# Holding each store that follows a load until the store ahead of it has landed on all DMA engines

## The chip, the cores and the metric

The kernel runs on one core of a Trainium2 chip. The metric is the device time of one execution in microseconds (us), lower is better.

## The reference, cut to what matters

```python
# q, k: (16 batches, 512 positions, 16 heads, 64) float32; cos, sin: (512, 32)
q_rot = concat([q1*cos - q2*sin, q1*sin + q2*cos], axis=-1)   # k_rot likewise
scores = np.einsum('bshd,bthd->bsht', q_rot, k_rot)           # (16, 512, 16, 512) float32
```

The output is 268.4 MB and the two inputs together are 67.1 MB. The arithmetic is small beside that, so the kernel is a stream of transfers with some matrix products behind it.

## The kernel before

One batch gives four stores of 4 MB each (128 positions x 16 heads x 512 columns), and needs one 2 MB load of q and one of k. All of them are issued by SyncE, in one queue, in the order store, q load, store, k load, store, store. Each store is split over 16 DMA engines (8 packets of 32 KB on each), each load likewise (8 packets of 16 KB).

```python
in_pool    = ctx.enter_context(tc.tile_pool(name="in", bufs=2))
stage_pool = ctx.enter_context(tc.tile_pool(name="stage", bufs=3))   # 3 x 4 MB: the stores' sources
...
def load(which, b):
    ...
    nc.sync.dma_start(t.rearrange("p c (h d) -> p c h d", h=H), dram[which][b])
...
def store(i, st):
    o = o_v[i // C, i % C]
    if i < NST - 1:
        nc.sync.dma_start(o, st)
        return
    ...                                # the last store of all goes in three pieces
...
for i in range(C, NST):                # C = 4 stores a batch, NST = 64 stores
    ...
    st = stage_pool.tile([P, H, S], fp32, tag="stage", name="st")
    for p in range(HP):
        scores(i, p, st)               # matmuls, copy to st; the last p calls store(i, st)
        ...
    if i % C == C - 2:
        load("q", i // C + 2)
    elif i % C == C - 1:
        load("k", i // C + 3)
```

In the text, s0 to s3 are the four stores of a batch. The q load is issued behind s2, the k load behind s3; so s3 follows the q load, and the next batch's s0 follows the k load.

## Time and profile before

| | before |
|---|---|
| median of 3 runs | 801.04 us (800.56 to 801.60) |
| profiled execution | span 799.0 us, clock 0.923 |
| bytes | 67.24 MB read, 268.44 MB written |
| DMA queue of the stores and loads | busy 98.6% of 16 engines' time |

The first two lines below are from the profile's page of the kernel before, its part on DMA issues: what is issued, how often, its size, and the median time from issue to landing. The last one is the page's row of GB/s in 40 equal slices of the span.

```profile
out_dram<-st SPq DMA_DIRECT2D x59, 4096.0 KB, 23.9
k_sb<-in_k_dram SPq DMA_DIRECT2D x15, 2048.0 KB, 26.9
...
GB/s 355 422 424 424 432 427 433 425 435 427 421 437 426 439 427 430 433 431 430 431 428 433 434 428 429 433 438 420 418 426 434 435 415 418 426 440 375 422 439 231
```

A 4 MB store at 432 GB/s takes 9.7 us, so a time to landing of 23.9 us means that a store stands behind more than a whole other transfer. The row of GB/s is even, 415 to 440 from the second slice to the 36th, and ends in a slice with 231: there some DMA engines have finished and others have not. The first and the last of the 16 DMA engines are 8.9 us apart at the end. This distance is called the **lead** here. The engine that is last sets the time.

Under these views lie two sorts of records. A transfer leaves 16 completion marks, one for each DMA engine; "first marks" and "last marks" below are the earliest and the latest of the 16. And each packet has a start and a duration. Where numbers come from these, the text says so, and tables made from them stand in ordinary fences.

### The profile page before, as it was taken

To read this page: it belongs to the slowest core of one execution; us is meant where nothing else is said; L and a number is where in the kernel's file an instruction comes from. 1 tells how busy PE (TensorE), PEld (TensorE's weight loads), DVE (VectorE), ACT (ScalarE), POOL (GpSimd) and SP (SyncE) were. 2 spreads that over 40 slices of the span, in tenths; PEclk is the share of its full clock that TensorE was granted. 3 is DMA by queue.
4 is the path that set the end of the run, shared out by engine and by line. 5 is a ranking of instruction groups with operands and counts; after the bars stand their busy time and mean duration, and the time that the engine had idled before them with its cause. 6 is when DMAs were issued, how large, how long until landed. Compare 5 with 4: busy or idle time off the path is not lost.

```text
span 799.0 us, 7715 instructions
## 1 busy us (share of the span) xinstructions
PE 691.3 (87%) x3072; PEld 299.3 (37%) x3072; DVE 544.6 (68%) x516; ACT 561.2 (70%) x647; POOL 0.7 (0%) x6
## 2 busy tenths in 40 slices
PE   4989998997979979799797997979979799799970
PEld 2444443343434334343343443424434343344420
DVE  6999987676866768577585775857758478585300
ACT  3888886775857758577585775757757677578870
POOL 0000000000000000000000000000000000000000
PEclk9999999898998989889898898988989899899995
DMA  9999999999999999999999999999999999998995
GB/s 355 422 424 424 432 427 433 425 435 427 421 437 426 439 427 430 433 431 430 431 428 433 434 428 429 433 438 420 418 426 434 435 415 418 426 440 375 422 439 231
DMA packets 17844, 336.17 MB, mean 421 GB/s; under 512 B 1808, under 2 KB 3088, under 8 KB 4240
## 3 DMA queue, kind: packets, MB, share of 16 engines
q1 hardware_dynamic: 17520, 335.55, 98.6%
q8 instruction: 24, 0.39, 0.2%
q10 hardware_dynamic: 288, 0.13, 0.1%
q14 instruction: 12, 0.10, 0.0%
HBM read 67.24 MB, written 268.44 MB: 420 GB/s over the span
## 4 chain that ended last, share of the span: by engine, by line
DMA 50%; PE 40%; ACT 4%; DVE 3%; issue 1%; ACTq 0%; SPq 0%; DVEq 0%
DMA out_dram<-st 47%; PE ps L166 30%; PE bank L127 10%; ACT st L173 4%; DMA q_sb<-in_q_dram 2%; DVE part L106 1%; DMA early<-in_k_dram 1%; DVE q_sb L107 0%; DVE k_sb L107 0%; DVE k_sb L111 0%; DVE q_sb L111 0%; DVE early L107 0%; DVE kT_t L142 0%; ACTq L281 0%; DVE early L111 0%
## 5 line engine op out<-in xcount | busy, mean ns | idle before, releaser
L173 ACT COPY st<-ps 128x1024 f32<-128x1024 f32 x512 | 494.7, 1018 | 203.7 <-DMA out_dram<-st 105.6
L166 PE MATMUL ps<-kT_t,qT_t 64*128 64x512 f32 x2048 | 548.9, 654 | 71.0 <-ACT st L173 70.9
L166 PEld LDWEIGHTS ps<-kT_t,qT_t 64*128 64x128 f32 x2048 | 185.0, 197 | 261.7 <-issue 144.6
L142 DVE COPY qT_t<-bank 128x512 f32<-128x512 f32 x118 | 81.6, 691 | 203.8 <-PE bank L127 203.8
L127 PEld LDWEIGHTS bank<-ident,q_sb 128*128 128x128 f32 x480 | 55.6, 152 | 102.5 <-issue 99.1
L127 PE MATMUL bank<-ident,q_sb 128*128 128x128 f32 x480 | 86.9, 308 | 0.9 <-PE ps L166 0.9
L127 PEld LDWEIGHTS bank<-ident,k_sb 128*128 128x128 f32 x480 | 50.5, 141 | 95.4 <-issue 38.7
L127 PE MATMUL bank<-ident,k_sb 128*128 128x128 f32 x480 | 78.7, 287 | 1.6 <-DVE qT_t L142 1.2
L142 ACT COPY kT_t<-bank 128x512 f32<-128x512 f32 x122 | 72.5, 599 | 6.4 <-PE bank L127 6.4
L107 DVE TENSOR_TENSOR q_sb<-q_sb,cos_t 128x1024 f32<-128x1024 f32 x60 | 73.5, 1226 | 2.1
L111 DVE TENSOR_TENSOR k_sb<-k_sb,part 128x1024 f32<-128x1024 f32 x60 | 73.5, 1225 | 2.1
L107 DVE TENSOR_TENSOR k_sb<-k_sb,cos_t 128x1024 f32<-128x1024 f32 x60 | 73.5, 1225 | 2.0
L106 DVE TENSOR_TENSOR part<-q_sb,ss_t 128x1024 f32<-128x1024 f32 x60 | 73.5, 1225 | 2.0
L106 DVE TENSOR_TENSOR part<-k_sb,ss_t 128x1024 f32<-128x1024 f32 x60 | 73.0, 1216 | 0.1
L111 DVE TENSOR_TENSOR q_sb<-q_sb,part 128x1024 f32<-128x1024 f32 x60 | 73.0, 1216 | 0.0
L127 PE MATMUL bank<-ident,early 128*128 128x128 f32 x64 | 10.5, 316 | 12.5 <-DVE early L111 10.6
L127 PEld LDWEIGHTS bank<-ident,early 128*128 128x128 f32 x64 | 8.3, 161 | 17.5 <-issue 13.4
L106 DVE TENSOR_TENSOR part<-early,ss_t 128x1024 f32<-128x1024 f32 x8 | 9.8, 1223 | 5.9 <-DMA early<-in_k_dram 5.8
L111 DVE TENSOR_TENSOR early<-early,part 128x512 f32<-128x512 f32 x16 | 10.3, 687 | 0.2
L107 DVE TENSOR_TENSOR early<-early,cos_t 128x1024 f32<-128x1024 f32 x8 | 9.8, 1225 | 0.3
L142 ACT COPY qT_t<-bank 128x512 f32<-128x512 f32 x10 | 5.7, 617 | 3.2 <-PE bank L127 3.2
L142 DVE COPY kT_t<-bank 128x512 f32<-128x512 f32 x6 | 4.1, 685 | 0.3 <-PE bank L127 0.3
(9 smaller groups left out, 2.8 us busy)
## 6 DMA issues: line engine op xcount, KB each, us to landing
out_dram<-st SPq DMA_DIRECT2D x59, 4096.0 KB, 23.9
k_sb<-in_k_dram SPq DMA_DIRECT2D x15, 2048.0 KB, 26.9
q_sb<-in_q_dram SPq DMA_DIRECT2D x15, 2048.0 KB, 29.9
out_dram<-st SPq DMA_DIRECT2D x16, 1024.0 KB, 14.3
out_dram<-st SPq DMA_DIRECT2D x1, 3584.0 KB, 20.4
early<-in_k_dram SPq DMA_DIRECT2D x1, 1536.0 KB, 8.9
early<-in_q_dram SPq DMA_DIRECT2D x1, 1536.0 KB, 12.1
early<-in_k_dram SPq DMA_DIRECT2D x1, 512.0 KB
```

Source lines behind the costliest of these rows:

```text
L106: nc.vector.tensor_tensor(pv, xs, ss, op=mult)
L107: nc.vector.tensor_tensor(xc, xc, cs, op=mult)
L111: nc.vector.tensor_tensor(y, y, z, op=add)
L127: nc.tensor.transpose(bank[:, x, :], src, ident)
L142: copy(out=dst, in_=src)
L166: nc.tensor.matmul(out=po, lhsT=lhs[64 * r : 64 * r + 64, :], rhs=rh, start=True, stop=True)
L173: nc.scalar.copy(out=so, in_=si)
```

## The change

The intent: the fast DMA engines run ahead of the slow one; if a store that follows a load waits until the store ahead of that load has landed on all 16, the lead can't grow, and the load that lies between keeps the slow engine busy during the wait. Nothing else is changed: 24 stores (s3 and s0 of batches 2 to 13) get one more condition.

```diff
+    HELD = [x for x in range(2 * C, NST - 2 * C) if x % C in (0, C - 1)]
...
+    stores = {}
+    held = mybir.DependencyInfo(mybir.DependencyClass.Sync, mybir.DependencyReason.ANTI)
+
     def store(i, st):
         o = o_v[i // C, i % C]
         if i < NST - 1:
-            nc.sync.dma_start(o, st)
+            stores[i] = nc.sync.dma_start(o, st)
+            if i in HELD:
+
+                tc.add_manual_dep(stores[i].ins, stores[i - 1].ins.name, held, reason="lead")
             return
```

## The prediction

> **What bounds the kernel now.** I read the page's strip of 40 slices and its DMA queues first, to see whether the transfers or the compute engines are full.
>
> ```profile
> PE   4989998997979979799797997979979799799970
> ...
> DMA  9999999999999999999999999999999999998995
> ...
> q1 hardware_dynamic: 17520, 335.55, 98.6%
> ```
>
> TensorE has holes (7s), the DMA row has none until slice 37. The transfers of the one queue take 98.6% of the time of 16 DMA engines: 335.55 MB in 799 us. So I asked next for the stretches (start:end, span of the stretch, then busy time of each engine; the last three numbers are the granted clock, the DMA share and GB/s).
>
> ```profile
> 400.00:600.00 200.00, 178.12 (x778) 75.96 (x778) 138.60 (x130) 141.10 (x162) 0.00 (x0) 0.91 1.00 429
> ...
> 730.00:780.00 50.00, 43.91 (x196) 18.25 (x194) 13.93 (x16) 39.12 (x43) 0.00 (x0) 0.97 0.98 420
> 780.00:799.00 19.00, 0.00 (x0) 0.00 (x0) 0.00 (x0) 0.00 (x0) 0.00 (x0) 0.56 0.57 236
> ```
>
> The middle is full of DMA (share 1.00). In the last 19 us nothing computes and only 57% of the DMA engines' time is used: some engines are done before others. That is the "lead" that the change speaks of. The timeline of the queue that issues the transfers shows one period (start, duration, what is issued), and the chain of waits shows what a period hangs on:
>
> ```profile
> 433.00 0.33 SPq L147 DMA_DIRECT2D out_dram<-st  x1
> 433.43 1.00 SPq L79 DMA_DIRECT2D q_sb<-in_q_dram  x1
> 449.23 0.33 SPq L147 DMA_DIRECT2D out_dram<-st  x1
> 449.66 0.56 SPq L79 DMA_DIRECT2D k_sb<-in_k_dram  x1
> 459.25 10.35 SPq L147 DMA_DIRECT2D out_dram<-st  x2
> ```
>
> ```profile
> 408.91 28.12 DMA out_dram<-st
> ...
> 437.12 1.02 ACT st L173
> 438.14 0.04 issue
> 438.19 2.08 PE ps L166 x4
> ...
> 458.21 1.02 ACT st L173
> 459.23 0.02 issue
> 459.25 27.26 DMA out_dram<-st
> ```
>
> A period is store, q load, store, k load, store, store. A 4 MB store lands 28.12 us after its issue, of which it needs about 10 to move: the rest it stands in line. Its landing frees one of three stage buffers, ScalarE and TensorE refill it, and the next store is issued at 459.25, long before the DMA engines can start it. The wait view says the same from the queue's side and from ScalarE's:
>
> ```profile
> SPq L147 <- ACT st L173: 657.0, 59, 16.6
> ...
> ACT st L173 <- DMA out_dram<-st: 105.6, 28, 6.0
> ```
>
> The queue is waiting for data 657 us in total, ScalarE waits 105.6 us for buffers, and neither leaves the DMA engines empty.
>
> Then I went below these views, to the trace's 16 completion marks of each transfer, one for each DMA engine, and to its packets. Three facts, all mine from those records:
> - The first and the last mark of a transfer drift apart: 3.67 us at the store issued at 73.85, 5.47 at 210.78, 9.19 at 408.91, 11.75 at 630.97, and 8.91 at the store issued at 777.43. Near the end, one engine alone makes most of it: of the store issued at 616.90 the last mark is 11.45 us after the first, the one before it 5.42.
> - Between stores the first marks are 9.68 us apart, the last ones 9.83 to 10.01; for a load it is about 4.86 us for the last mark. Of 6,251 full 32 KB packets between 100 and 700 us, most took 1.213 us. Those between 1.216 and 1.30 us follow each other without a gap nearly all the time: one DMA engine, about 34 ns longer in each of the eight packets of a store (0.27 us a store).
> - Four stores and two loads on the slow engine: last marks at 437.02 and 486.51, 49.5 us apart. 4 x 9.96 + 2 x 4.86 = 49.6. So **the slow engine is never empty, and its work is the end of the kernel**.
>
> **What the Trainium skill says.** "DMA: Bandwidth & Descriptors", section "Why a DMA increments its semaphore by 16 and not by 1": the engines of one DMA finish independently, and only the full 16 means that all has landed. The trace agrees: 16 marks, up to 11.75 us apart. The same page, "Anatomy of one DMA": a DMA engine does not wait on a semaphore, the wait happens on the issuing sequencer before dispatch, and a DMA has a fixed cost of about 2 us. The first holds here (the queue's waits above); the fixed cost measures less: the store issued at 740.24 found an engine just run dry and its first mark came at 751.19, 10.95 us later; less 9.68 of moving that is 1.27 us, of which 0.48 lie between the end of the last packet (436.54) and the mark (437.02). Same page, "Where 436 GB/s comes from": 16 ports give 435 GB/s, 27.2 each. 32 KB in 1.213 us is 27.0 GB/s: the fast engines run at their own ceiling, so slowing them down hands nothing obvious to the slow one.
>
> **The change part by part.** It removes and moves no instruction; the order on every engine is the same. It adds one condition to 24 stores (two of each batch, stores 8 to 55): the whole landing of the store before.
> 1. *What the queue waits.* In the kernel before, a store after a q load was ready a mean of 7.9 us, and one after a k load 12.8 us, before the last mark of the store ahead (nine of each whose marks are complete). So all 24 will really be held: 12 x 7.9 + 12 x 12.8 = 248 us of waiting on the issuing queue. In that time the queue would mostly have waited for ScalarE.
> 2. *What the slow engine sees.* When the last mark comes, it has the 2 MB load queued already (issued 0.43 us after the store, some 24 us before it is needed). It needs 4.86 us for it. From its last packet's end to the first packet of the held store: 0.48 (mark) + 0.8 (the rest of the 1.27) + some 0.1 of waking = 1.4 us. Reserve: 4.86 - 1.4 = about 3.5 us. **No bubble on the slow engine**: cost 0 of 24 x 1.4 = 34 us.
> 3. *What the fast engines see.* They finish the load ahead of the slow one and run dry if their lead is over about 3.5 us. So the lead is cut to about 3.5 us at each held store. They lose up to 10 us once in the course of the run, which they lose in the kernel before too: in the tail, and at about 550 and 650 us, where the lead fell from 11.7 to 10.0.
> 4. *What follows behind.* The k load, issued right after the held store, slips by 8 us, but stands behind that store anyway. The store after a held one: I drew the buffers by hand, with the landing of the batch's first store as 0. Landings 0, 10, 20, 35, 50, 60, 70; a buffer is refilled 10 us after it comes free; the store that lands at 60 is ready at 30 and may be issued at 35, the one that lands at 70 at 45. Both are there well before 50 and 60. Cost 0.
> 5. *What could be gained.* The slow engine's excess: 63 large stores x 0.27 = 17 us at the very most, an estimate. But its excess does not grow with the lead: it is there at 83 us already, with a lead of 3.7. It follows TensorE instead: a mean of 12 ns a packet where TensorE was busy under a quarter of the packet's time, 35 ns where it was over three quarters; and 39 against 30 ns with over half of the engines in a load against none. The change thins such overlap out: at most 87 packets x 10 ns = 0.9 us.
>
> Sum: 801.04 + 0 - 0.5 = **800.5 us**.
>
> **The rivals.** *(a) The lead itself makes the slow engine slow*, so cutting it gives back up to its excess; for it speaks the tail with 43% of the DMA time empty, against it that the excess is there at small leads. It would make 788 to 796 us; I give it one in ten. *(b) The held stores leave the slow engine empty*, because waking, issuing and starting take longer than one load: each microsecond over 4.86 costs 24 us. A wait of 6 us would make 828. Against it the 1.27 us measured; one in twenty-five. *(c) TensorE or ScalarE becomes the bound* as buffers come free later: 178 us of 200 busy leaves TensorE 11%, and buffers come free with the slow engine as before. Under 2%.
>
> **Range and chances.** My case leaves 0 to 1 us of gain; run to run the kernel moves by 0.5. For (a) in part I go down to 794, for a little of (b) up to 805. Over 2% faster means under 785, which needs nearly all of the slow engine's excess gone: 0.03. Over 2% slower, over 817, needs 0.7 us of emptiness at every held store: 0.03. The rest, 0.94, is the same.
>
> **What would show each step.** (1) The queue's wait view: a new line, stores waiting for stores, about 24 times and 200 to 250 us. (2) Issue to landing: held stores at about 15 us (4.86 - 0.5 + 10), k loads at about 19 instead of 26.9, q loads still near 30; the DMA share in the middle still about 1.0. (3) First and last mark of a transfer never much over 4 us apart at held stores, growing by some 2 us in the last eight stores. (5) Last marks still 9.9 to 10.0 us apart between stores. The prediction is wrong if the last marks move to 9.7 us (rival a), or if packets on the slow engine show gaps before held stores (rival b).

## More of the kernel before

The marks of each transfer are told apart by counting them off from the front, 16 for each; only the last two, small transfers leave fewer. So a mean over the 12 batches rests on all twelve, of the one execution that was profiled.

## The result, and the profile after

| | before | after |
|---|---|---|
| median of 6 runs | 801.11 us (800.17 to 801.68) | 806.02 us (805.08 to 806.95) |
| ratio | | 1.0062 (95%: 1.0049 to 1.0075) |
| profiled span, clock | 799.0 us, 0.923 | 804.7 us, 0.925 |

The first three of the six runs before are those of the table above. A ratio is the mean time of one kernel's fast runs over the mean of the other's fast runs of the same rounds, so it is not quite the ratio of the medians quoted. The changed kernel is 4.9 us, or 0.6%, slower. By the 2% rule that is "the same", but it lies outside the predicted range, and the interval excludes zero.

**The page after.** The rows are the DMA busy tenths and the GB/s in 40 slices, the share of the queue, and the issue-to-landing medians.

```profile
DMA  9999999999999999999999999999999999999997
GB/s 358 423 424 429 435 424 422 417 429 433 404 435 415 418 437 398 435 420 414 424 410 431 418 417 433 403 433 423 410 429 404 431 419 416 430 421 424 437 426 301
...
q1 hardware_dynamic: 17520, 335.55, 99.1%
...
out_dram<-st SPq DMA_DIRECT2D x59, 4096.0 KB, 21.2
k_sb<-in_k_dram SPq DMA_DIRECT2D x15, 2048.0 KB, 19.7
q_sb<-in_q_dram SPq DMA_DIRECT2D x15, 2048.0 KB, 28.6
```

The change did what it was meant to do: the last slice has 301 GB/s where it had 231, so the engines finish closer together, and the DMA queue is busier than before (99.1% against 98.6%). Yet the same bytes took longer. Busy DMA engines that move less: between the second slice and the 36th, the row of GB/s has dips to 398 to 410 that the kernel before doesn't have. It isn't emptiness but slowness, and that is the reading to take from this page.

**The stretches after** (start:end, span, busy time of PE, PEld, DVE, ACT, POOL; then clock, DMA share, GB/s).

```profile
100.00:400.00 300.00, 266.59 (x1164) 113.81 (x1164) 208.60 (x196) 211.84 (x243) 0.00 (x0) 0.91 1.00 422
...
400.00:600.00 200.00, 173.48 (x776) 74.37 (x774) 136.76 (x129) 140.46 (x163) 0.00 (x0) 0.92 1.00 421
...
780.00:804.70 24.70, 0.94 (x6) 0.11 (x2) 0.00 (x0) 2.50 (x3) 0.00 (x0) 0.62 0.78 329
```

In the middle, 421 GB/s at a DMA share of 1.00; before, the stretch 400 to 600 had 429, also at 1.00. In the tail, 78% of the DMA engines' time is used, before it was 57%.

**The queue's timeline after** (start, duration, issue), one period, and **the chain of waits after** over the same time:

```profile
409.64 0.33 SPq L151 DMA_DIRECT2D out_dram<-st  x1
410.08 1.91 SPq L80 DMA_DIRECT2D k_sb<-in_k_dram  x1
424.48 9.45 SPq L151 DMA_DIRECT2D out_dram<-st  x3
434.03 1.14 SPq L80 DMA_DIRECT2D q_sb<-in_q_dram  x1
459.86 0.33 SPq L151 DMA_DIRECT2D out_dram<-st  x1
```

```profile
385.17 24.41 DMA out_dram<-st
...
409.64 14.77 DMA out_dram<-st
424.42 0.02 issue
...
433.59 26.20 DMA out_dram<-st
...
459.86 14.74 DMA out_dram<-st
```

The store issued at 409.64 is a held s3; it lands 14.77 us later, and only then, at 424.48, the held s0 goes out, together with two that had been ready. In the chain of before a store took 27 to 28 us from issue to landing; now the held ones take 14.5 to 15.6, by the marks of all 24.

**The queue's waits and ScalarE's, after** (who waits for whom: us in total, times, longest):

```profile
SPq L151 <- DMA out_dram<-st: 446.2, 24, 24.6
SPq L151 <- ACT st L180: 214.6, 25, 11.3
```

```profile
ACT st L180 <- DMA out_dram<-st: 114.2, 33, 6.6
```

The first line is the change: 24 waits of a store for a store. The two lines together are 660.8 us, where the kernel before waited 657.0 for ScalarE alone: the hold lies inside a wait that was there already. Counted from the end of the last copy into a store's buffer to the store's issue, the 24 holds come to 271 us (before: under 1 us). ScalarE waits 8.6 us longer for its buffers.

**Where the time went.** The last marks, from the trace, give the speed of the engine that sets the end. The table has the mean distance from the last mark of one transfer to the last mark of the next, in us, and in brackets the same for the first marks:

```
            q load       s3            k load        s0           s1           s2            period
before   4.91 (4.91)  9.97 ( 9.87)  4.93 (5.03)  9.89 (9.70)  9.82 (9.68)  10.01 ( 9.68)  49.53 (48.88)
after    5.07 (4.94)  9.90 (10.33)  5.33 (5.06)  9.86 (9.77)  9.86 (9.69)   9.90 (10.15)  49.94 (49.95)
```

The four stores together became 0.17 us faster on the last engine (39.70 to 39.53), the two loads 0.57 us slower (9.84 to 10.41), 0.41 of it in the k load. The sum, 0.40 us a period, times 12 periods is 4.8 us of the 5.2 by which the last mark of the last held store (store 55) comes later (719.46 before, 724.68 after); the other 0.4 us was there at store 7, before the first hold. The last mark of the last store's large piece is 5.24 us later. So nearly all of it was lost before the tail, and nothing came back in the tail although the lead there is 5.5 us instead of 8.9: a shorter lead let the fast engines finish later, not the slow one earlier.

**What happens at a load.** The rate of all engines in half-microsecond steps, worked out from the packets, at the same place of both kernels:

```
us         418.0  418.5  419.0  419.5  420.0  420.5  421.0  421.5  422.0
before       431    430    432    431    432    432    432    432    433   GB/s
after        431    431    343    324    322    311    379    425    428   GB/s
```

At 419 the changed kernel's engines, which the hold had made run dry and then released together at 410, finish the held store and turn to the k load. Eleven packets of 32 KB that start between 419.02 and 419.68 take 1.4 to 2.4 us each where 1.21 is usual. The view of stretches shows the same dip; the first two lines are the kernel before, the last two the changed one:

```profile
419.00:421.00 2.00, 2.00 (x12) 0.72 (x8) 1.35 (x3) 0.00 (x0) 0.00 (x0) 1.00 1.12 483
421.00:423.00 2.00, 0.20 (x2) 0.00 (x0) 1.00 (x1) 0.67 (x1) 0.00 (x0) 1.00 1.08 467
...
419.00:421.00 2.00, 2.00 (x12) 1.11 (x12) 1.97 (x2) 1.76 (x4) 0.00 (x0) 1.00 1.03 328
421.00:423.00 2.00, 2.00 (x13) 0.81 (x9) 1.42 (x2) 0.82 (x1) 0.00 (x0) 1.00 1.02 434
```

This view counts a packet, its time and its bytes, where it starts, so in stretches as short as these only the ratio of GB/s to share tells how fast packets move: 483 / 1.12 = 431 before, 328 / 1.03 = 318 after, and 434 / 1.02 = 425 two us later. Nobody is idle, many are slow. The two kernels differ in step, too: before, the fast engines read while the slow ones still write (at 419.0, 234 GB/s of reads and 198 of writes). After, ten of the stretched packets start within 0.15 us of each other.

The slow engines themselves are hit later: at 624.49 the held s0 goes out, the fast engines start it together at about 625.7, and of the three or four engines that are still in their k load, seven packets take 0.7 to 1.4 us instead of 0.61 between 625.5 and 627.7. In the twelve batches in order the k load's last mark is 4.82, 4.87, 4.85, 5.82, 5.50, 5.39, 5.63, 5.15, 5.56, 5.41, 5.65 and 5.33 us after the store's: not in the first three, and in all nine from store 19 on. Loads are now and then this long without any hold, too, in the first third of a run: a q load of 5.55 and a k load of 5.27 in the kernel before. What makes those long is open.

### The profile page after: what moved, and what is told of

Its sections match the earlier page's. It is cut to its first block, busy times and chain, and to the rows that moved or that the text cites. A ratio compares the mean times of both kernels' runs of the same rounds, so it can differ in the third digit from the quotient of the medians.

```text
span 804.7 us, 7713 instructions
## 1 busy us (share of the span) xinstructions
PE 688.3 (86%) x3072; PEld 298.3 (37%) x3072; DVE 544.5 (68%) x516; ACT 561.5 (70%) x647; POOL 0.7 (0%) x6
## 3 DMA queue, kind: packets, MB, share of 16 engines
q1 hardware_dynamic: 17520, 335.55, 99.1%
## 4 chain that ended last, share of the span: by engine, by line
DMA 60%; PE 26%; DVE 5%; ACT 5%; issue 1%; ACTq 0%; SPq 0%
DMA out_dram<-st 59%; PE ps L173 20%; PE bank L128 7%; ACT st L180 5%; DVE part L107 2%; DVE early L112 1%; DVE k_sb L112 1%; DVE k_sb L108 1%; DVE early L108 1%; DMA sin_t<-in_sin_dram 0%; DVE kT_t L143 0%; DVE q_sb L108 0%; DVE q_sb L112 0%; ACT kT_t L143 0%; ACTq L288 0%
## 5 line engine op out<-in xcount | busy, mean ns | idle before, releaser
L128 PE MATMUL bank<-ident,early 128*128 128x128 f32 x64 | 10.5, 316 | 12.3 <-DVE early L112 10.4
## 6 DMA issues: line engine op xcount, KB each, us to landing
k_sb<-in_k_dram SPq DMA_DIRECT2D x15, 2048.0 KB, 19.7
q_sb<-in_q_dram SPq DMA_DIRECT2D x15, 2048.0 KB, 28.6
```

What stands on the lines that cost most here:

```text
L128: nc.tensor.transpose(bank[:, x, :], src, ident)
```

## The experiments

Twelve kernels ran, all with right results. Edits are against the changed kernel except where the text says so. Times before are those of the same rounds.

### two_back: the condition without its bite

```diff
-                tc.add_manual_dep(stores[i].ins, stores[i - 1].ins.name, held, reason="lead")
+                tc.add_manual_dep(stores[i].ins, stores[i - 2].ins.name, held, reason="lead")
```

> The same 24 stores are held, but for the landing of the store two before them, which in the kernel before had landed 2 us or more ahead of their issue. The wait stands in the program and never binds. Theories A, B and C: no change, 800.5 to 801.7, leads of 8 to 12 us as before. If the added semaphore wait itself cost time on the issuing queue, this run would be slower too, by some of the 5 us.

Measured: 801.08 us against 800.86, ratio 0.9994 (0.9974 to 1.0014). The queue's waits of this run:

```profile
SPq L151 <- ACT st L180: 411.8, 59, 13.7
SPq L151 <- DMA out_dram<-st: 245.1, 24, 15.0
```

The condition is waited on 24 times, and the sum of the two lines, 656.9 us, is that of the kernel before. So a condition more on 24 stores costs nothing. It also teaches a caution: a line of 245.1 us looks like a large new wait and is none, because the records put the wait for the data under the name of the condition as well.

### q_only and k_only: half of the holds

```diff
-    HELD = [x for x in range(2 * C, NST - 2 * C) if x % C in (0, C - 1)]
+    HELD = [x for x in range(2 * C, NST - 2 * C) if x % C == C - 1]     # q_only: s3, behind the q load
+    HELD = [x for x in range(2 * C, NST - 2 * C) if x % C == 0]         # k_only: s0, behind the k load
```

> Only the 12 stores after a q load are held; stores after a k load go as before. Theory A (the hold gathers some 12 engines into one crowd with a lead of 3.4 to 4.4 us over the late engines; when the crowd switches together, the 2 MB load that the late engines are still reading is stretched, above all the k load, by about 0.4 to 0.8 us a period): the lead at the k load is the same as with both holds, so the k load's last mark stays at 5.2 to 5.6 us after the one before it and the time is 804 to 806 us. Theory B (a fixed bubble of about 0.2 us on the slow engine at each of 24 held stores): half of the loss, about 803.5, and no stretched k load. Theory C (the k load is stretched because the held store and the next one are issued 0.43 us apart while it is being read): the stretch is gone, 801 to 802.

> Only the 12 stores after a k load are held. Theory A: the lead is cut to 3.5 us at the store after the k load and grows to about 4.6 us until the next k load; there is less overlap between the late engines' k load and the crowd's switch, so a smaller loss, 802 to 805 us, with a k load of 4.9 to 5.3 us. Theory B: half of the loss, about 803.5, k load at 4.86. Theory C: the full loss, 805 to 806, k load at 5.3 or more.

Measured: q_only 813.99 us, ratio 1.0161 (1.0138 to 1.0183); k_only 812.92 us, ratio 1.0141 (1.0119 to 1.0164). No text expected that **half of the holds cost almost three times as much as all of them** (13 and 12 us against 4.9). The last marks show where it sits:

```
            q load   s3     k load   s0     s1     s2     period
before       4.91   9.97    4.93    9.89   9.82  10.01    49.53
q_only       4.91   9.94    6.02    9.88   9.84   9.94    50.52
k_only       5.88   9.92    4.86    9.93   9.87  10.03    50.49
```

In each, one load is stretched by about 1 us, and it is the *first load after the hold*: the k load where s3 is held, the q load where s0 is. The other load and the stores are as before. Twelve times that is about the loss. The stretches of q_only in steps of 2 us show two dips around one load:

```profile
421.00:423.00 2.00, 2.00 (x10) 0.91 (x12) 1.93 (x3) 1.91 (x4) 0.00 (x0) 1.00 0.76 328
423.00:425.00 2.00, 2.00 (x12) 0.78 (x8) 1.97 (x2) 1.58 (x3) 0.00 (x0) 1.00 1.08 336
425.00:427.00 2.00, 2.00 (x10) 0.72 (x8) 1.35 (x3) 0.00 (x0) 0.00 (x0) 1.00 0.98 410
427.00:429.00 2.00, 0.03 (x2) 0.00 (x0) 0.83 (x1) 0.30 (x1) 0.00 (x0) 1.00 1.03 344
429.00:431.00 2.00, 1.24 (x4) 0.50 (x4) 0.00 (x0) 2.00 (x3) 0.00 (x0) 0.69 0.92 246
```

GB/s over share is 432, 311, 418, 334 and 267 in the five lines; the first one is no dip, it only has fewer packets that start in it. I worked out the rate in half-microsecond steps from the packets as well: the first dip, 305 to 330 GB/s, is at 423.5 to 425.5, the switch from store to load. The second, 217 to 304 GB/s, is at 428.5 to 431, the load's end, where s0, already queued, follows. In the second one 15 packets of 16 KB that are under way at the same time (at 429.95), so on 15 of the 16 engines, take 1.0 to 1.8 us. In the changed kernel s0 is held and doesn't stand behind the load, and the rate at this place falls no lower than 394 GB/s (425.5 to 427). That gave the next idea: the hold makes the fast engines run dry and start together (a **restart**); the first load after a restart is slow, and a store queued behind it makes it slower still.

### once: one hold

```diff
+    HELD = [27]
```

> A single store (27, after a q load) is held. Theory A: at that point the lead falls from about 7.7 to 3.4 us, and the k load right behind it and perhaps one or two more are stretched until the lead has grown past 4.9 us (about 1 us a period); then 4.86 us again. Time 801.3 to 802.5. Theories B and C: one event of 0.2 to 0.5 us at most, 801.1 to 801.6, and no load but the one next to the hold is stretched.

Measured: 802.37 us, ratio 1.0016 (0.9995 to 1.0036). The k load right behind store 27 took 6.20 us on the last mark; the other k loads take 4.71 to 4.92. At the next two loads the lead is still only 4.1 and 4.4 us, and they are not stretched (4.81 and 4.85); after that it grows again. So a short lead by itself need not cost anything: here one restart cost about 1.3 us, once. One q load of this run, in the first batch of the twelve and so without a restart, took 5.90 us, and two_back, whose holds never bind, has k loads of 5.37 to 5.86 in three of its first four batches. So a long load alone doesn't prove a restart; that every hold of q_only and k_only that has a load behind it is followed by one (5.5 to 6.6 us) is the stronger evidence.

### pair: one hold, and the next store held too

```diff
+    HELD = [27, 28]
```

> One hold (store 27) as in once, and the next one (store 28) as well, so that nothing stands in line behind the k load that follows the restart. If the store queued behind that load makes the second and larger half of the dip, the k load is 5.3 to 5.7 us instead of 6.2, its stretched 16 KB packets come to 3 to 6 us of engine time instead of 19, and the time is 0.3 to 1 us below that of once (802.4). If the queue behind the load does not matter: 6.0 us or more, 802.4 or above.

Measured: 801.68 us, ratio 1.0011 (0.9993 to 1.0028); the time tells nothing at this size, the trace does. The k load behind store 27 took 4.92 us (6.20 in once). Added up over all engines, its 16 KB packets were 5.9 us longer than usual (19.0 in once); the 32 KB packets at the switch were 8.6 us longer (9.2 in once). So the second dip, and with it nearly all of what the last engine loses at this load, comes from a store queued behind the first load after a restart. The second hold is a restart, too, and the next q load, which has a store queued behind it, took 5.57 us: part of the gain is lost again there. This explains why two holds in every batch cost less than one: each takes away the store behind the load that the other made slow.

### loose: a hold at a longer lead

Here s1 waits, on the landing of the k load two transfers ahead of it, so the lead may grow to about 9 us.

```diff
+    HELD = [x for x in range(2 * C, NST - 2 * C) if x % C == 1]
...
+        loads[which, b] = nc.sync.dma_start(t.rearrange("p c (h d) -> p c h d", h=H), dram[which][b])
...
+                tc.add_manual_dep(stores[i].ins, loads["k", i // C + 2].ins.name, held, reason="lead")
```

> The two holds of a batch are replaced by one that covers more: the second store of a batch (the one behind the first store after the k load) is held for the landing of the k load, so that a 4 MB store (9.7 us), not a 2 MB load (4.86 us), is queued ahead of the slow engine. Theory D (what costs is that the crowd of fast engines, restarted together by a hold, makes the transfer rate dip when it switches to its first load afterwards and back, and that the slow engine is in its own load during a dip as long as the lead is under about 4.9 us): the lead is bounded at about 8.3 us, dips occur once the bound binds (after about 390 us), but they fall into stores of the slow engine, its loads stay at 4.86 us, and the time is 800.5 to 802.5. Rival E (any restart of the crowd costs the slow engine about 1.2 us, at whatever lead): 7 or 8 binding holds, 806 to 812 us. Rival F (cutting the lead is worth something by itself): under 799.

Measured: 806.17 us, ratio 1.0048 (1.0022 to 1.0074), with one run of six at 799.87 and five from 804.23 to 807.47. The lead is bounded at 8.3 to 9.1 us, but the bound makes engines run dry only from about 430 us on. From there s2 takes 10.5 to 10.8 us on the last mark in five of six batches (in the sixth it is s1 that is long) and the q load 5.4 to 5.7. So a restart costs the last engine about 1 us at a lead of 8 to 9 us as well; that a long lead makes it harmless, because the slow engine is then elsewhere, fell. One oddity stays: the last marks of the other stores are 9.66 to 9.76 us apart from there on, not 9.9. That fits an engine without the longer packets that fell behind at loads (an inference: the packets don't name their engine). So "the slow engine" need not be one fixed cause in all executions.

### uncovered: a hold with nothing to do behind it

```diff
+    HELD = [x for x in range(2 * C, NST - 2 * C) if x % C == 1]
```

s1 waits for s0, directly ahead of it: no load lies between, so all 16 engines run dry. This measures the bubble that the prediction reckoned at 1.4 us.

> The second store of each batch is held for the landing of the store directly ahead of it, 12 times, with nothing queued between them. This measures the bubble that the prediction put at 1.4 us and said was covered by the load. All engines run dry: 12 x 1.4 = 17 us at least, 818. Theory D adds a dip at the first load afterwards (the q load, with the next store queued behind it), which now meets all 16 engines with a lead near 0: 12 x 1.1 to 1.4 = 13 to 17 us more, 831 to 835. If dips need a lead, or do no harm where all engines switch together, 816 to 820.

Measured: 855.92 us against 800.72, ratio 1.0685 (1.0671 to 1.0699): 55 us, or 4.6 for each of 12 holds, more than expected. The stretches over the middle, and the queue's waits:

```profile
100.00:700.00 600.00, 499.37 (x2156) 210.39 (x2152) 385.09 (x362) 392.62 (x450) 0.00 (x0) 0.91 0.94 390
```

```profile
SPq L151 <- DMA out_dram<-st: 372.8, 12, 33.1
SPq L151 <- ACT st L180: 329.8, 35, 17.8
```

Here, and only here of the kernels with holds alone, the DMA share falls (0.94). From issue to first mark a held store took 10.93 to 10.96 us: less 9.68 of moving, a bubble of 1.3 us from issue, as predicted. On the last marks s1 was mostly 11.2 or 13.1 us behind s0, by turns; where it was 11.2, s2 took 11.7. Together s1 and s2 took 3.0 us more than in the kernel before, so the bubble is less than half of that; the rest I didn't follow up. The q load, the first after the restart, took 6.1 to 7.7 us (mean 6.73), the k load behind it 4.83 to 5.08, although the 16 engines are then hardly further apart. So it is again the first load that is hit, and the second one that is not.

### q_tiny, tiny_only, q_stagger, q_fan: can a small load take the blow?

If the first load after a restart is slow whatever its size, a tiny one might clear the way. In q_tiny an 8 KB load carries the hold of q_only, ahead of the held store; tiny_only has the same loads without a hold.

```diff
+    tiny = const_pool.tile([P, 16], fp32, name="tiny")
...
+                t = nc.sync.dma_start(tiny, cos.rearrange("(p c) j -> p c j", c=C)[:, 0, :16])
+                tc.add_manual_dep(t.ins, stores[i - 1].ins.name, held, reason="lead")     # not in tiny_only
+            stores[i] = nc.sync.dma_start(o, st)
```

> As q_only (813.99 us, first load after each hold stretched to 6.3 us and the last packets of the store ahead of it stretched too), but an 8 KB load into an unused tile goes ahead of each held store and carries the hold. Theory S (a restart leaves something in the engines that the first load afterwards, of whatever size, clears; the second load after a restart was never stretched): the k load is the second load now and stays at 4.86 us; the time is that of tiny_only plus 0 to 1.5 us, some 801.5 to 804. Theory T (what dips the rate is that the engines run aligned in time to 0.2 us after the restart): the tiny load does not undo the alignment, the k load stays near 6.3 us, 813 to 817.

> Control: the 12 tiny loads at the same places with no hold. All theories: 801 to 803.5 (12 times 0.05 to 0.2 us on each engine), k loads at 4.86 us.

Measured: q_tiny 819.45 us, ratio 1.0224 (1.021 to 1.0237); tiny_only 802.19, ratio 1.0011 (0.9997 to 1.0024). The k load of q_tiny still takes 5.9 to 6.8 us on the last mark. The tiny load clears nothing, and the theory that the first load of any size does fell.

Over the loads of all these runs, the dip goes with how closely the fast engines keep step: where ten engines started their packets of the store ahead within 0.2 us, the 32 KB packets at the switch were mostly 4 to 12 us longer in sum, and where it was 0.3 us or more, mostly not at all, with exceptions on both sides. That is a correlation. q_stagger (a small load on 119 rows, so on some of the engines) and q_fan (four of them on different row counts) were to spread the restart out.

```diff
+                t = nc.sync.dma_start(tiny[:119], dram["q"][0, :119, 0, :4])                # q_stagger
+                tc.add_manual_dep(t.ins, stores[i - 1].ins.name, held, reason="lead")
...
+                for x, rows in enumerate((104, 100, 119, 116)):                             # q_fan
+                    t = nc.sync.dma_start(tiny[x][:rows], dram["q"][0, :rows, 0, 0])
+                    if x == 0:
+                        tc.add_manual_dep(t.ins, stores[i - 1].ins.name, held, reason="lead")
```

> As q_tiny (819.45 us, ratio 1.0224, k loads of 6.2 to 6.8 us), but the small load ahead of each held store has 119 rows of 1 KB, so that it should use only 7 of the 16 engines, 17 rows each, and delay those by 0.5 to 0.8 us behind the others. Theory T (engines that restart within 0.2 us of each other switch from store to load together, and that makes the rate dip): the restart now comes in two groups, fewer than 10 engines within 0.2 us; the stretched 32 KB packets ahead of the k load fall from 8 to 11 us of engine time to 0 to 5, the k load to 4.9 to 5.8 us, the time to 804 to 814 (the delay itself may cost up to 12 x 0.7 us if the slow engine is among the 7). If alignment is not the cause: k loads as in q_tiny and 819 us or more.

> As q_tiny, with four small loads of 104, 100, 119 and 116 rows of 256 B ahead of each held store in place of one, meant to use 13, 10, 7 and 4 engines, so that the restart is spread over about 1 to 2 us and no 9 engines start within 0.15 us (in q_stagger 9 still did, and the dip stayed). Only the trace counts; the loads themselves cost time, 815 to 840 us. Theory T (alignment at the restart makes the dip): the stretched 32 KB packets ahead of the k load fall from 8 to 11 us of engine time to under 4. If they stay at 8 or more, alignment is not what carries the effect from the restart to the first load, and that stays open.

Measured: q_stagger 825.99 us, ratio 1.0308 (1.0294 to 1.0322). The engines started in two groups, nine within 0.14 us and six some 0.7 us later, and the dip stayed: 32 KB packets of 2.0 to 2.4 us. q_fan, one look of unknown state: 828.35 us; the small loads were over before the store came, the engines still started within 0.2 to 0.3 us, and the dip stayed. So I could not spread the engines far enough, and whether their keeping step is the cause is not settled.

### relief: what the slow engine's share is worth

On the kernel before, store 40 goes in two pieces, rows 0 to 119 and 120 to 127, to give the last engine less of the first one.

```diff
+            if i == 40:
+                nc.sync.dma_start(o[:120], st[:120])
+                nc.sync.dma_start(o[120:], st[120:])
+                return
```

> The kernel before, without any hold; the store number 40 alone is issued as two, rows 0 to 119 and rows 120 to 127, so that the last of the 16 engines moves nothing of the first and probably nothing of the second. It tests whether one slow engine sets the end. If that engine is the slow one, it is 9.7 us less behind: last marks of later stores close to the others, the lead near the end 2 to 5 us instead of 11, and 793 to 797 us. If another engine is the slow one, or if the end is set by something else: 801 to 802.5.

Measured: 818.8 us, ratio 1.0225 (1.0212 to 1.0238), 18 us slower by one split store. The page counts 7 packets more than before (17527), which is what marks from 15 engines for the one piece and 8 for the other, in place of 16, would give (an inference). From 515 to 540 us the DMA share was 1.00 at only 335 GB/s: 42 packets of 32 KB took 2.4 to 5.1 us there where 1.21 is usual. So packets can also be slow without any restart. The lead jumped from 9.4 to 15.5 and then 23.6 us, and engines stood partly empty after it:

```profile
540.00:550.00 10.00, 0.34 (x2) 0.00 (x0) 1.14 (x2) 0.00 (x0) 0.00 (x0) 0.64 0.99 395
550.00:560.00 10.00, 7.97 (x30) 3.53 (x32) 4.71 (x5) 6.88 (x8) 0.00 (x0) 0.68 0.80 316
```

The experiment did another thing than it was meant to, so its question, what one engine's relief is worth, was not answered.

## Why the prediction was wrong

**Step 1, what the queue waits: right in kind.** All 24 stores are held, and the hold lies inside the wait for ScalarE (657.0 against 660.8 us in sum). Counted as the prediction did, from the moment when the data is ready, the holds are 271 us where it had 248. Its sign, a line of 200 to 250 us in the wait view, was wrong: the line has 446.2, because the record counts the wait for the data too, as two_back shows.

**Step 2, no bubble on the slow engine: right; its 4.86 us for the load: wrong.** The last marks at the held stores are 9.90 (s3) and 9.86 (s0) us behind those of the load ahead, before 9.97 and 9.89. Held stores land in 14.5 to 15.6 us (15 predicted), k loads in 19.7 (19), q loads in 28.6 (near 30), and the DMA share stays 1.00. But the k load takes 5.33 us and the q load 5.07 where the step has 4.86 for either, for the reason that step 3 left out. The bubble where nothing covers it is 1.3 us from issue, as reckoned. Rival (b), empty slow engines, is excluded for the changed kernel.

**Step 3, the fast engines run dry harmlessly: this failed.** The lead was cut as predicted (2.9 to 4.4 us at stores 8 to 55, 5.5 at the end). But the sentence that the fast engines "run dry" and lose only "what they lose in the kernel before too" left out how they come back. At their next switch from a store to a load the rate of all engines falls from 432 to 311 GB/s for about 2 us, and when they start the next store together, the late engines' k load is stretched. In place of 0 this costs the last engine 0.57 us in the two loads of a period; the stores give 0.17 back. The prediction had drawn from the engines' ceiling of 27 GB/s that slowing some "hands nothing obvious" to another. That was beside the point: it didn't ask whether stopping and restarting some can *take* something from another.

**Step 4, what follows behind: right as far as seen.** s1 and s2 take 9.86 and 9.90 us on the last marks, before 9.82 and 10.01; ScalarE's 8.6 us of longer waits for buffers show nowhere on them.

**Step 5, the gain: too small in size, and swallowed.** At most 0.9 us was reckoned; the stores' last marks suggest 12 x 0.17 = 2.0 us (an estimate, since the last engine need not be the same one all the time). Rival (a), that the lead makes the slow engine slow, is excluded in the size it was given (5 to 13 us): the longer packets are there at a lead of 4 us too, and the time went up.

**Rival (c)**, TensorE or ScalarE as the bound, didn't happen: between 400 and 600 us TensorE is busy 173 us of 200, less than before (178).

The right sum would have been 801.1 + 12 x 0.40 = 805.9, against 806.0 measured. What the runs show: a hold makes engines restart, the first load after the restart is slow, and a store queued behind that load makes it slower. What they leave **open**: why engines restarted together dip at that switch, whether their keeping step is the cause, what carries the state from the hold through the whole store to its end some 9 us later, why the stretch of the k load begins only at the fourth of twelve batches, why single loads early in a run are long without a restart, and why one engine's 32 KB packets are 34 ns longer.

No version beat the kernel before; two_back, tiny_only, once and pair are level with it.

## What to carry to other kernels

When DMA engines that run at their ceiling drift apart, the drift itself may be worth keeping: a wait for all of them can cost more than the bubble it makes. Here the bubble was hidden, and the first load after the restart paid. Before such a hold is added for a better end, look at the row of GB/s beside the DMA share: a share of 1.00 with fewer GB/s (421 against 429 here, over 200 us) is slowness, which no count of idle time shows. And if a hold is needed ahead of a load, don't let the next store stand in the queue behind that load: pair against once is 1.3 us less for that one load, though 0.8 us more for the load after the second hold.

## What the Trainium skill lacked or had wrong

- **No page has the restart dip.** "DMA: Bandwidth & Descriptors", section "Where 436 GB/s comes from", gives a ceiling of 435 GB/s, and the even rate here, 432, comes near it. It has no word on engines started together: 432 falls to 311 GB/s for about 2 us at the first switch from store to load, and to 217 to 304 with a store queued behind the load.
- **No fixed cost for a DMA that SyncE issues.** The same page, "Anatomy of one DMA", has about 2 us for a DMA, for the path through GpSimd alone; it has no such sum for SyncE. Here, issued by SyncE, from issue to first mark a 4 MB store on empty engines took 10.93 to 10.96 us, of which 9.68 is moving: 1.3 us.
- **What a split by rows can cost.** No page has the size of such a loss: 818.8 us against 800.72 here, for one 4 MB store cut into 120 and 8 rows, with 32 KB packets of up to 5.1 us where 1.21 is usual.
- **One engine that is slower for stores only.** The same page, "Latency and other measured facts", has two engines that are usually slower and guesses at the rings of the GpSimd path. Here, without that path, the 32 KB store packets of what looks like one engine take about 1.25 us instead of 1.213, and no difference is seen in its loads (4.86 us on the last mark).
